# A branch prefetch hint in TensorE's stream ahead of each branch over an expert's further tiles

## The chip, the cores and the metric

The kernel runs on one core of one Trainium2 chip. The metric is the device time of one execution in microseconds (us), as the median of several runs. Five engines run their own instruction streams and meet through semaphores: TensorE (PE; its weight loads are shown apart as PEld), VectorE (DVE), ScalarE (ACT), GpSimd (POOL) and SyncE (SP, which issues most DMAs). A "q" behind an engine's name (PEq, DVEq) means its sequencer, which branches and signals and feeds the engine.

## What is computed

One layer of a decoder trunk over 2,048 tokens of width 1,024: a mixer of three kinds of heads, and then a mixture of 16 experts, of which each token uses two. The change lies in the experts:

```python
def hierarchical_moe(h, w_rg, b_rg, w_re, b_re, w_gate, w_up, w_down):
...
    top_p, top_local = lax.top_k(expert_prob, TOP_K)
    weights = group_p * top_p / jnp.sum(top_p, axis=-1, keepdims=True)
    expert_idx = group_idx * EXPERTS_PER_GROUP + top_local
...
    for e in range(N_EXPERTS):
        hidden = jax.nn.silu(h @ w_gate[e]) * (h @ w_up[e])
        y = y + combine[..., e:e + 1] * (hidden @ w_down[e])
    return y
```

The result goes through a gate and a residual sum, and a last RMS norm. How many tokens an expert gets is known only when the router has run.

## The kernel before

The first 1,155 us or so are the mixer, the output projection and the router. The router writes, for each expert, a list of its tokens to memory, and loads the 16 counts (and four counts of groups) into registers of every engine (`nreg`). Then come the experts, one after the other, in tiles of 128 tokens.

`body(e)` (L1275) computes the first two tiles of expert e without any condition. For each tile the token rows are gathered by an indirect DMA on GpSimd (`gather`, L814) into a buffer `xg`, turned by eight transposes on TensorE (`x_T`, L1195) and split into a high and a low part (`xh`, `xl`) on ScalarE and VectorE. `gates(e, t)` (L1245) multiplies them with the gate and up weights: 8 slices of the width, three products each, 24 products of 128x512 (L53) into a bank `pv` or `sc`. ScalarE and VectorE make `hid` of it, `split_h` (L1200) turns and splits that into `hh` and `hl`, and `down` (L1214) does 12 products with the down weights. The sums go to memory by an indirect scatter-add on GpSimd (`add`, L1226), whose index tile is `PI` or `PC` (both are columns of `PIC`). The last expert has its own order (`last_body`, L1334). `gates` takes an optional function `middle`, which it calls ahead of the products of slice `MID_K`, 6; its instructions then stand between the 18th and the 19th product.

`chain(e, t)` (L1399) does the tiles from the third on (t = 2 and up), if the expert has so many tokens: a condition on the count at L1403 holds the whole tile and, nested in it, the condition for the next tile, down to the 16th. Every engine takes the branch. In TensorE's program the 14 nested bodies stand one behind the other, some 95 instructions each (a product is two, the weight load and the matmul), behind them 14 short exits, one for each condition not met (a semaphore step that makes up for what the body would have signalled, and a jump), and then what follows. An expert that has no third tile so jumps from its first branch over some 1,350 instructions. An expert with more tiles falls through once per tile, and then jumps from inside the chain; its exit ends in a second, short jump over the other exits. Here experts 4, 5, 6, 8, 10 and 11 have more than two tiles (two more for 4, three for 8, one for the others), and the other ten jump at once. `fin_chain` is a chain of the same kind over the tokens of a group.

The scheduler moves work over the conditions where nothing forbids it. So the first 14 of the 24 products of the next expert's first tile stand ahead of the branch of this expert. Which of them stay behind is told by `LATE_K` and `behind`. All of this is the same in both programs.

## Time and profile before

| what | us |
| --- | --- |
| median of 3 runs (1643.43 to 1652.88) | 1648.55 |
| the profiled execution | 1652.45 |
| its span | 1650.6 |
| TensorE busy in the span | 1429.5 |
| VectorE busy | 1116.4 |
| ScalarE busy | 763.6 |
| GpSimd busy | 591.8 |

The span is the time from the first to the last instruction of the program; what lies around it makes up the rest of the execution. Times of day below, such as 1240.23, are microseconds from the span's start. An engine's idle time is given in square brackets behind the instruction that ended it, with what that instruction had waited for. "issue" stands where it waited for nothing that the profile shows. The experts' stage is the stretch from about 1155 us on.

### The profile page before, as it was taken

How to read it: one execution, taken by the hardware profiler on the slowest of the kernel's cores; microseconds unless marked ns; L12 is line 12 of the kernel's file. 1: busy time of each engine (PE TensorE's matmuls, PEld its weight loads, DVE VectorE, ACT ScalarE, POOL GpSimd, SP SyncE). 2: the span in 40 equal slices, each digit the busy share in tenths (PEclk: the TensorE clock that was granted, in tenths of full speed). 3: DMA queues.
4: the chain of work that ended last, by engine and by line, in shares of the span. 5: the costliest groups of instructions: out<-in, count | busy, mean ns of one | idle time of the engine just before them, and what ended most of it. 6: DMA issues, size and time to landing. Idle time of an engine off the chain costs nothing. (4 is left out here: it accounts for less than half of the span.)

```text
span 1650.6 us, 23125 instructions
## 1 busy us (share of the span) xinstructions
PE 1429.5 (87%) x6896; PEld 1142.4 (69%) x6896; DVE 1116.4 (68%) x3072; ACT 763.6 (46%) x1537; POOL 591.8 (36%) x618
## 2 busy tenths in 40 slices
PE   4899999989998689889979999995899997999881
PEld 4777797777787366667757777784677775777660
DVE  5767656556556798968737887887464566466664
ACT  4373235645555478778742332223243353334331
POOL 4100133011233444545342344444342335435453
PEclk9899999999999899999988999995999998999985
DMA  9448861355668755243242443234786668587845
GB/s 315 143 123 291 299 227 71 102 154 162 171 183 233 196 152 129 70 135 106 71 149 90 141 146 135 103 107 126 222 227 156 174 198 255 118 269 220 270 98 178
DMA packets 177097, 277.07 MB, mean 168 GB/s; under 512 B 31161, under 2 KB 120265, under 8 KB 176864
## 3 DMA queue, kind: packets, MB, share of 16 engines
q1 hardware_dynamic: 151184, 212.33, 41.0%
q0 software_dynamic: 25680, 62.09, 14.0%
q8 instruction: 90, 1.47, 0.4%
q14 instruction: 143, 1.17, 0.2%
HBM read 209.90 MB, written 89.03 MB: 181 GB/s over the span
## 5 line engine op out<-in xcount | busy, mean ns | idle before, releaser
L53 PE MATMUL sc<-R,R 128*128 128x512 f32 (+1 forms) x1352 | 328.1, 394 | 14.7 <-ACT R L128 5.6
L53 PEld LDWEIGHTS sc<-R,R 128*128 128x128 f32 x1352 | 250.0, 192 | 77.0 <-DVE fmx L272 8.3
L53 PE MATMUL sc<-R,yh 128*128 128x512 f32 x512 | 171.9, 416 | 19.6 <-DVE x L923 13.4
L53 PEld LDWEIGHTS sc<-R,yh 128*128 128x128 f32 x512 | 95.9, 195 | 44.2 <-DVE x L923 18.7
L814 POOL DMA_INDIRECT xg<-h_d,LT x55 | 63.3, 1151 | 167.1 <-PEq L1403 50.4
L129 DVE TENSOR_TENSOR ptlo<-tp,pthi 128x512 fp32r<-128x512 f32 (+3 forms) x163 | 99.3, 624 | 25.7 <-ACT pthi L128 24.9
L53 PE MATMUL sc<-R,fq 128*128 128x512 f32 (+3 forms) x320 | 97.5, 404 | 16.8 <-DVE fmx L272 6.4
L128 ACT ACTIVATE pthi<-tp 128x512 fp32r<-128x512 f32 (+3 forms) x163 | 85.5, 546 | 52.6 <-PE tp L293 25.6
L53 PE MATMUL sc<-R,hh 128*128 128x512 f32 x328 | 102.7, 415 | 7.6 <-ACT hh L128 5.0
L53 PE MATMUL sc<-R,yl 128*128 128x512 f32 x256 | 103.9, 407 | 0.0
L53 PE MATMUL pv<-R,xh 128*128 128x512 f32 x256 | 88.2, 424 | 13.2 <-PEq L1403 12.9
L923 DVE SCALAR_TENSOR_TENSOR x<-sc,r,x 128x512 f32<-128x512 f32 x96 | 71.7, 747 | 36.3 <-PE sc L53 28.6
L53 PE MATMUL pv<-w,xh 128*128 128x512 f32 x256 | 85.6, 411 | 9.5 <-PEq L1403 5.8
L282 POOL TENSOR_SCALAR row<-row,frs 128x640 f32<-128x640 f32 (+11 forms) x48 | 66.7, 1391 | 48.3 <-DVE frs L281 31.8
L293 PEld LDWEIGHTS tp<-ident,row 128*128 128x128 f32 x504 | 63.0, 142 | 26.3 <-issue 10.5
L293 PE MATMUL tp<-ident,row 128*128 128x128 f32 x504 | 79.9, 277 | 0.9 <-DVE fmx L278 0.5
L129 DVE TENSOR_TENSOR R<-R,R 128x512 fp32r<-128x512 f32 (+1 forms) x122 | 78.9, 699 | 0.0
L128 ACT ACTIVATE xh<-tp 128x512 fp32r<-128x512 f32 x82 | 45.3, 596 | 71.9 <-PE tp L1195 68.5
L128 ACT ACTIVATE R<-R 128x512 fp32r<-128x512 f32 (+1 forms) x130 | 73.1, 644 | 7.6 <-POOL R L1342 5.2
L53 PEld LDWEIGHTS sc<-R,fq 128*128 128x128 f32 x320 | 54.2, 197 | 32.3 <-DVE fmx L272 9.7
L53 PEld LDWEIGHTS sc<-R,hh 128*128 128x128 f32 x328 | 61.7, 196 | 21.0 <-ACT hh L128 5.6
L280 ACT ACTIVATE row<-row,fmx 128x640 f32<-128x640 f32 (+11 forms) x48 | 68.0, 1417 | 13.7 <-DVE fmx L278 9.9
(394 smaller groups left out, 3533.3 us busy)
## 6 DMA issues: line engine op xcount, KB each, us to landing
x<-in_x SPq DMA_DIRECT2D x32, 512.0 KB
x<-in_w_mod SPq DMA_DIRECT2D x32, 512.0 KB
R<-in_w_gate SPq DMA_DIRECT2D x128, 128.0 KB
R<-in_w_up SPq DMA_DIRECT2D x128, 128.0 KB
R<-in_w_down SPq DMA_DIRECT2D x32, 512.0 KB
wraw<-in_w_inT SPq DMA_DIRECT2D x24, 512.0 KB
R<-kc_d SPq DMA_DIRECT2D x80, 128.0 KB
wm<-in_w_mod SPq DMA_DIRECT2D x32, 256.0 KB
```

The costliest lines, as they stand in the source:

```text
L53: return PE.matmul(o, l, r, start=first, stop=last)
L128: return (ACT.activation(hi, src, AF.Copy), (lo_eng or V).tensor_tensor(lo, src, f32(hi), op=ALU.subtract))
L129: (lo_eng or V).tensor_tensor(lo, src, f32(hi), op=ALU.subtract))
L280: ACT.activation(row[:, 0:n], row[:, 0:n], AF.Exp, bias=ng, accum_out=rs)
L282: G.tensor_scalar(row[:, 0:n], row[:, 0:n], rs, 1.0, op0=ALU.mult, op1=ALU.mult)
L293: PE.transpose(p[:, r * 128:(r + 1) * 128], rows[r][:, j * 128:(j + 1) * 128], ident)
L814: return G.indirect_dma_start(out=dst, out_offset=None, in_=h2_d[:, :], in_offset=bass.IndirectOffsetOnAxis(ap=idx, axis=0), **(dict(bound ...
L923: V.scalar_tensor_tensor(x1[:, sl], p, r3s[t][:, g:g + 1], x1[:, sl], op0=ALU.mult, op1=ALU.add)
```

## The change

A new helper `hint(label)` puts a branch prefetch hint into TensorE's stream, for a branch that carries a label. Each condition of `chain` gets a label, `more{e}_{t}`. The hint says "LikelyTaken". For the first condition of an expert it is put into `gates(e, 1)`, the products of the second tile, at the place of `middle`. For the others it stands at the head of the body around them. The conditions of `fin_chain` and the other engines get none.

```diff
@@ body
-            gates(e, 1)
+            gates(e, 1, lambda: hint(f"more{e}_2"))
@@ last_body
-            a = gates(e, 1)
+            a = gates(e, 1, lambda: hint(f"more{e}_2"))
@@ tile_kernel
+        def hint(label):
+            tc.mark_branch_hint_location(label, "LikelyTaken", engines=[_mybir.EngineType.PE])
+
         def chain(e, t):
...
-                with tc.If(nreg[e] > t * 128):
+                with tc.If(nreg[e] > t * 128, label=f"more{e}_{t}"):
+                    if t < NT - 1:
+                        hint(f"more{e}_{t + 1}")
                     if t > 2 and e < NE - 1:
```

On TensorE, in the products of expert 0's second tile (`pv` from `R`, `xh` and `xl`): the piece of the difference around the first hint.

```order
 L53 MATMUL pv<-R_11399,xh_11721 128x512
 L53 MATMUL pv<-R_11395,xl_11724 128x512
+L1550 BRANCH_PREFETCH_HINT
 L53 MATMUL pv<-R_11396,xh_11721 128x512
 L53 MATMUL pv<-R_11400,xh_11721 128x512
```

One instruction is new, between the 18th and the 19th of the 24 products; nothing else moves. From here to the branch stand 6 products of this tile, 2 transposes of `hid`, 12 products of `down`, 8 transposes of `x_T` and 14 products of the next expert: 42.

On TensorE, at the branch of expert 0 (`w` are the next expert's weights, `xg` and `hid` belong to the third tile): the difference at the first condition and the head of its body.

```order
 L53 MATMUL pv<-w_11750,xh_11720 128x512
 L53 MATMUL pv<-w_11754,xh_11720 128x512
-L1403 COMPARE_AND_BRANCH
+L1406 COMPARE_AND_BRANCH
+L1550 BRANCH_PREFETCH_HINT
 L1195 MATMUL tp<-ident,xg_11726 128x128 x8
 L1203 MATMUL tp<-ident,hid_11743 128x128 x2
```

The branch stands where it stood (its line is now L1406), and the hint for the next condition comes right behind it, the first instruction of the body. Over the whole program TensorE has 224 rows more, all of them hints; the other four engines have the same rows in the same order.

## Rows read from the trace of the kernel before

**Rows 1.** Busy time of each engine in two stretches, up to the experts and in them. The columns are PE, PEld, DVE, ACT and POOL busy (and their instructions), the granted TensorE clock, the DMA share and GB/s.

```profile
0.00:1155.00 1155.00, 1018.23 (x5061) 821.15 (x5062) 829.32 (x2450) 581.23 (x1163) 391.27 (x472) 0.94 0.50 155
...
1155.00:1640.00 485.00, 411.31 (x1837) 321.25 (x1835) 287.13 (x623) 182.40 (x376) 200.50 (x147) 0.93 0.70 203
```

**Rows 2.** Waits of TensorE from 1155 to 1640 us: who waited for whom, us in total, times, the longest.

```profile
PE pv L53 <- PEq L1403: 20.8, 14, 3.2
PE tp L1203 <- DVEq L1403: 9.0, 2, 6.6
PE sc L53 <- DVE hl L129: 8.0, 5, 3.3
...
PE sc L53 <- ACT hh L128: 5.0, 2, 4.5
```

**Rows 3.** Line 1403 on TensorE's sequencer over the whole span: the branches with their shortest, median and longest time in ns; and the engine that waited longest for them, in us and times.

```profile
L1403 PEldq COMPARE_BRANCH  x31: 65/3363/7258, 1164.6 to 1625.1; - x31
...
  POOL xg L814: 50.4, 6
```

**Rows 4.** The same line in short windows that hold one branch each: its time in ns and its start. They belong to experts 3, 4 (three branches), 7, 9 and 13.

```profile
L1403 PEldq COMPARE_BRANCH  x1: 6981/6981/6981, 1233.1 to 1233.1; - x1
...
L1403 PEldq COMPARE_BRANCH  x1: 70/70/70, 1257.1 to 1257.1; - x1
...
L1403 PEldq COMPARE_BRANCH  x1: 65/65/65, 1266.8 to 1266.8; - x1
...
L1403 PEldq COMPARE_BRANCH  x1: 4023/4023/4023, 1276.9 to 1276.9; - x1
...
L1403 PEldq COMPARE_BRANCH  x1: 7238/7238/7238, 1364.6 to 1364.6; - x1
...
L1403 PEldq COMPARE_BRANCH  x1: 6390/6390/6390, 1446.4 to 1446.4; - x1
...
L1403 PEldq COMPARE_BRANCH  x1: 5902/5902/5902, 1557.7 to 1557.7; - x1
```

**Rows 5.** The DMA queue q8, which brings TensorE's instructions: packets, MB and share of the DMA engines, over the span, up to 1155 us, and from 1564 to 1569.4 us.

```profile
q8 instruction: 90, 1.47, 0.4%
...
q8 instruction: 40, 0.66, 0.2%
...
q8 instruction: 1, 0.02, 1.0%
```

**Rows 6.** Timeline of TensorE at the jumps of experts 0 (two rows), 3, 7, 9 and 13: start, duration, operation, count, and in brackets the idle time before it.

```profile
1166.93 0.63 PE L53 MATMUL pv<-w,xh 128*128 128x512 f32 x2
1169.68 0.47 PE L53 MATMUL pv<-w,xl 128*128 128x512 f32 x1 [2.13 <-PEq L1403]
...
1240.23 0.48 PE L53 MATMUL pv<-R,xh 128*128 128x512 f32 x1 [2.92 <-PEq L1403]
...
1372.03 0.47 PE L53 MATMUL pv<-R,xh 128*128 128x512 f32 x1 [3.19 <-PEq L1403]
...
1452.97 0.47 PE L53 MATMUL pv<-R,xh 128*128 128x512 f32 x1 [2.21 <-PEq L1403]
...
1563.79 0.47 PE L53 MATMUL pv<-R,xh 128*128 128x512 f32 x1 [1.72 <-PEq L1403]
```

**Rows 7.** The same at the jump of expert 1 (the last row ahead of it and the first behind it) and at the exit of expert 4.

```profile
1195.49 0.40 PE L53 MATMUL pv<-R,xl 128*128 128x512 f32 x1
1196.04 0.48 PE L53 MATMUL pv<-R,xh 128*128 128x512 f32 x1
...
1281.67 0.50 PE L53 MATMUL pv<-w,xh 128*128 128x512 f32 x1 [0.44 <-PEq L1403]
```

**Rows 8.** The same at the 19th and 20th product of expert 0's second tile.

```profile
1156.80 0.63 PE L53 MATMUL pv<-R,xh 128*128 128x512 f32 x2
```

**Rows 9.** Timeline of GpSimd, VectorE and TensorE around the first products of expert 8: a scatter-add is issued, VectorE waits to write its index tile again, and TensorE waits for VectorE.

```profile
1363.13 1.56 POOL L1226 DMA_INDIRECT x_d<-yc,PIC  x1 [0.30 <-issue]
...
1373.26 0.15 DVE L1316 COPY PIC<-PIC 128x1 int32<-128x1 int32 x1 [8.69 <-DMA x_d<-yc,PIC]
...
1379.10 0.66 PE L1203 MATMUL tp<-ident,hid 128*128 128x128 f32 x2 [6.59 <-DVEq L1403]
```

**Rows 10.** The chain that ended last, in order of time, behind the jump of expert 14: start, us, what.

```profile
1598.01 1.54 PE tp L1195 x8
...
1599.67 1.04 POOL xg L814
```

**Rows 11.** Timeline of TensorE a few products behind the jumps of experts 13 and 14.

```profile
1569.31 0.58 PE L53 MATMUL pv<-R,xl 128*128 128x512 f32 x1 [4.59 <-issue]
...
1595.40 0.50 PE L53 MATMUL pv<-w,xh 128*128 128x512 f32 x1 [2.51 <-issue]
```

**Rows 12.** Busy time in five short stretches, with the columns of rows 1; the granted clock is the third number from the end.

```profile
1240.80:1244.20 3.40, 3.40 (x14) 2.83 (x13) 0.90 (x2) 1.04 (x3) 2.79 (x3) 0.50 0.55 154
...
1517.30:1520.70 3.40, 3.40 (x10) 2.63 (x11) 0.58 (x2) 0.44 (x2) 2.79 (x3) 0.50 0.13 16
1541.20:1544.60 3.40, 3.40 (x9) 2.30 (x10) 0.42 (x1) 0.44 (x2) 0.00 (x0) 0.50 0.53 193
1565.10:1575.30 10.20, 5.99 (x19) 4.91 (x19) 3.24 (x6) 3.37 (x7) 2.70 (x3) 0.50 0.30 111
1595.80:1599.20 3.40, 3.40 (x14) 2.90 (x13) 1.03 (x5) 1.58 (x4) 0.00 (x0) 0.50 0.10 34
```

## The prediction

> The timeline tells what such a wait costs TensorE [rows 6]. Branches of 6.98, 7.24, 6.39 and 5.90 us (experts 3, 7, 9, 13) leave TensorE idle 2.92, 3.19, 2.21 and 1.72 us: each time about 4.1 us less. That is the work queued ahead of the branch when the sequencer reaches it. The first branch leaves 2.13. An exit of 4.02 us, at expert 4, leaves only 0.44 us: there the cover is enough, and 0.44 is what the exit's semaphore step and its second, short branch cost anyway [rows 4, 7].

> **The change part by part.** It adds 224 hints, on TensorE alone; no other engine's instructions move. 25 are executed: 16 in the second tile's products and 9 at the head of a body that runs (31 branches, less 16 long exits, less 6 short second branches at experts 4, 5, 6, 8, 10 and 11, are 9 that fell through). 16 of them name a branch that is taken, 9 one that isn't.

> *The hint itself.* No row of before shows one. The nearest is a sequencer instruction that goes nowhere, the branch not taken at 65 to 70 ns: 25 x 0.07 = 1.8 us of the sequencer, which runs some 4 us ahead of TensorE [rows 4, 6]. I take 0; the bounds are 0 and 1.8. Without that cover it would cost the 1.8.

> *Is it early enough?* Between the hint and the branch of an expert stand 42 products. TensorE starts the first of them at 1156.80 for expert 0, and the last two ahead of the jump at 1166.93 [rows 8, 6]: 10.1 us for a fetch that took at most 7.3. In a body the hint stands right behind one branch, and the next branch comes 9.7 us later (1257.1, 1266.8) [rows 4]. So a fetch that starts at the hint, or even 2.4 us behind it, is in place.

> *What goes.* All the exposed time down to what a near jump leaves. That floor is 0.44 us for the six exits from inside a chain, and about 0.15 for the eight others (expert 1, whose wait is wholly covered, has one product end at 1195.49 + 0.40 and the next start at 1196.04) [rows 7]. 20.8 - 6 x 0.44 - 8 x 0.15 = 17.0 us. Bounds: 0 (the hint does nothing) and 17.0.

> *What is late next.* Behind expert 7's branch TensorE waits 6.59 us for VectorE, which sat 8.69 us on the landing of a scatter-add that GpSimd had issued at 1363.13, before that branch [rows 9]. This wait doesn't move with TensorE, so the 3.0 us of that branch (3.19 - 0.15) come back as a longer wait: -14.0 left. For the others I see the queued work follow TensorE: GpSimd's gathers behind the branch wait 50.4 us for TensorE's sequencer [rows 3], and the chain that ended last goes through TensorE's transposes behind expert 14's branch and the gather that they release [rows 10].

> *The code that moves.* Two more holes carry the name "issue": 4.59 us at 1569.31 and 2.51 us at 1595.40 [rows 11], a few products behind the jumps of experts 13 and 14. In the first, one packet of q8 falls between jump and the hole's end [rows 5]: the block behind the target is not there yet. TensorE had run 10,123 instructions in 40 blocks by 1155 us [rows 1, 5], 253 each. The holes put a block's end some 12 and 3 instructions behind the two targets. In the changed program 196 and 210 more instructions stand ahead of these, which puts the next block's end some 70 and 45 behind the targets. At 0.23 us a pair of weight load and product that is 8 and 5 us of work, as long as most fetches. Both holes should close: -7.1 us. Other jumps come nearer to a block's end (expert 6, from some 115 to some 20 instructions), for which I give back 2. Taken: -5; bounds -7.1 and +2 (the two holes only move to other experts).

> *The clock.* [...] The bounds are 0 (the clock falls elsewhere) and -9.8. I take -6, as idle times of up to 6.6 us for VectorE stay.

> *Sum.* -14.0 - 5 - 6 = -25. TensorE has 22 us of other waits in the stage (9.0 + 8.0 + 5.0, and small ones) [rows 2]; I let 3 come back through them. So -22 us. The profiled execution took 1652.45 us (its span 1650.6), which becomes 1630.45. The median of the three runs is 1648.55, 3.9 lower; the gain is a difference within one execution, so I set it against the median: 1648.55 - 22 = 1626.5.

> **The rivals.**
> *A. The hint fetches nothing of use* (it is ignored, or it fetches the place where the branch falls through, which comes next anyway). Branches stay at 3.4 to 7.3 us, and only the moved code counts: 1648.55 - 5 = 1643.5, from 1641.5 to 1650.5. For it: no row shows a hint, and the body is the branch's "true" side. Against it: nothing in the rows.
> *B. The jumps get short, but what follows isn't ready.* Besides expert 7's, the holes of experts 0 and 3 are followed by waits of 3.3 us (for hl, the longest of its line) and 2.4 us (the smaller of the two on VectorE's queue) [rows 2]. If these only grow, the 2.0 and 2.8 us of those holes come back too, and with clock and code as before -14.0 + 4.8 = -9.2 is left, or 1639.5. Against it: VectorE's part ahead of both starts from TensorE's transposes.
> *C. Slower: the block that a hint fetches takes the place of the one that comes next.* Counted in blocks of some 255 instructions, a block's end lies between hint and branch at experts 0, 1, 2, 3 and 12 of the ten that jump at once, and nine hints are wrong. Each of these 14 then has a fetch more in its way. At the five, the second fetch finds the queued work already used up, and costs near the middle of 3.4 and 7.3 us [rows 3], say 5: +25. The nine find their 4.1 us of cover: +1 each, +9. The jumps that still win give -9, the moved code -5: +20, or 1668.5. It decides against the change once the 14 cost more than 14 us together, 1 us each. For it: up to 1155 us the trace has one block per 253 instructions, so no row shows that more than the next one is kept [rows 5]. Against it: in 9.7 us between hint and branch there is time for two fetches one behind the other.
> [...]

> **How the numbers follow.** Forecast 0.60, A 0.16, B 0.12, C 0.12. A measurement of this kernel can tell about 0.5%, 8.2 us, from no change: faster is below 1640.3, slower above 1656.8. Faster: 0.56 of the forecast, 0.03 of A (its lower end with a little of the jumps), 0.06 of B, together 0.65. Slower: 0.11 of C and 0.01 of A, 0.12. The rest, 0.23, is within. The range: the forecast's own bounds are 1648.55 - 17.0 - 7.1 - 9.8 = 1614.6 below, and B's 1639.5 above. I reach up to 1650 to hold A, and down to 1612, and leave out C and a little of the forecast's edge.

> **What would show it.** In the profile after, right: the 16 exits at L1406 take 0.1 to 0.3 us, TensorE's wait for its sequencer there falls from 20.8 to under 5 us, q8 has more packets than 90 (nine wrong hints), no "issue" hole of over 2 us stands behind experts 13 and 14, and fewer stretches have a clock of 0.50. A: the exits keep their 3.4 to 7.3 us. B: short exits, but the waits for hl and on VectorE's queue grow by as much. C: exits and "issue" holes that together cost more than the 20.8 + 7.1 us of now. I am wrong if the exits are short and the stage from 1155 us on still takes as long.

## The result and the profile after

The changed kernel took 1658.70 us (median of 8 runs, 1651.24 to 1661.05) against 1648.7 of the kernel before on the same chip: 1.0058 times its time, interval 1.0037 to 1.0079. The forecast was 1626.5, with a range up to 1650. The profiled execution took 1659.7 us, its span is 1657.3.

The waits of TensorE in the experts' stage (1155 to 1645 us; who waited for whom, us in total, times, the longest) answer to [rows 2]:

```profile
PE tp L1203 <- DVEq L1406: 24.2, 8, 10.9
PE sc L53 <- DVE hl L129: 11.6, 4, 5.1
PE tp L1203 <- DVE hid L1263: 6.6, 1, 6.6
PE pv L53 <- ACT xh L128: 5.9, 4, 5.3
PE sc L53 <- ACT hh L128: 5.1, 3, 4.0
PE pv L53 <- PEq L1406: 5.1, 8, 2.3
...
PE pv L53 <- issue: 0.2, 1, 0.2
```

Read the sixth row first: the wait for TensorE's own sequencer, 20.8 us before, is 5.1. The "issue" holes of [rows 11] are gone too (7.1 to 0.2). But the wait for VectorE's sequencer at the same branch has grown from 9.0 us to 24.2, and those for hl, hid and xh have grown as well (from 8.0, 3.5 and 1.4 us). All rows of this view add to 63.8 us, where those of before add to 60.1: TensorE is idle for longer than before, for other engines.

The branch's line over the whole span, and who waited for it (us, times), against [rows 3]:

```profile
L1406 PEldq COMPARE_BRANCH  x31: 69/327/6477, 1165.0 to 1630.5; - x31
...
  PE tp L1203: 24.2, 8
...
  DVE hid L1263: 5.9, 1
```

The same line in windows that hold experts 3, 4, 7, 9 and 13, against [rows 4]:

```profile
L1406 PEldq COMPARE_BRANCH  x1: 327/327/327, 1237.8 to 1237.8; - x1
...
L1406 PEldq COMPARE_BRANCH  x3: 69/78/338, 1258.7 to 1278.7; - x3
...
L1406 PEldq COMPARE_BRANCH  x1: 350/350/350, 1368.6 to 1368.6; - x1
...
L1406 PEldq COMPARE_BRANCH  x1: 6477/6477/6477, 1450.8 to 1450.8; - x1
...
L1406 PEldq COMPARE_BRANCH  x1: 364/364/364, 1561.6 to 1561.6; - x1
```

So here the hint does what it says: 14 of the 16 exits take 0.33 to 0.38 us, and the 16 together 13.3 us, after 81.4. Expert 0's took 1.86 us, and expert 9's stayed at 6.48. The packets of q8 over the span and from 1247.0 to 1258.6 us, and those of q14, the other queue that the profile calls "instruction", answer to [rows 5]:

```profile
q8 instruction: 81, 1.33, 0.3%
...
q8 instruction: 1, 0.02, 0.5%
...
q14 instruction: 144, 1.18, 0.2%
```

That q8 serves TensorE is read from the trace of before: in each of the 16 long branches falls a packet of q8, of 16,384 bytes. Queue q8 moved fewer packets than before, 81 after 90, although nine hints are wrong; q14 moved 143 before. At expert 4 one packet comes behind the first hint, at 1251.6, none from the second hint (1258.8) to the branch of the exit, and this branch, at 1278.7, takes 338 ns. I read this as one fetch that served all three hints: the exit blocks of one expert lie close together in the program.

Where some of the time went is to be seen at expert 7, in the timelines of GpSimd, VectorE and TensorE, against [rows 9]:

```profile
1367.14 1.56 POOL L1226 DMA_INDIRECT x_d<-yc,PIC  x1 [0.30 <-issue]
...
1378.55 0.15 DVE L1316 COPY PIC<-PIC 128x1 int32<-128x1 int32 x1 [9.97 <-DMA x_d<-yc,PIC]
...
1384.38 0.66 PE L1203 MATMUL tp<-ident,hid 128*128 128x128 f32 x2 [10.93 <-DVEq L1406]
```

TensorE's hole of 3.19 us at this exit is gone, and the one behind it is 10.93 us, not 6.59. That much the prediction had. What it had not is on the other engines. The next four fences give the same line, 1403 or 1406, in ScalarE's program at expert 3's exit and in VectorE's at expert 13's, in a second trace of the kernel before and in the changed kernel: the branch, and the first semaphore step in the block that it jumps to, each with its start at the end of the row.

```profile
L1403 ACTq COMPARE_BRANCH  x1: 45/45/45, 1230.1 to 1230.1; - x1
L1403 ACTq EVENT_SEMAPHORE  x1: 17/17/17, 1230.8 to 1230.8; - x1
```

```profile
L1406 ACTq COMPARE_BRANCH  x1: 45/45/45, 1228.6 to 1228.6; - x1
L1406 ACTq EVENT_SEMAPHORE  x1: 17/17/17, 1231.2 to 1231.2; - x1
```

```profile
L1403 DVEq COMPARE_BRANCH  x1: 63/63/63, 1554.8 to 1554.8; - x1
L1403 DVEq EVENT_SEMAPHORE  x1: 21/21/21, 1555.6 to 1555.6; - x1
```

```profile
L1406 DVEq COMPARE_BRANCH  x1: 56/56/56, 1561.8 to 1561.8; - x1
L1406 DVEq EVENT_SEMAPHORE  x1: 21/21/21, 1567.7 to 1567.7; - x1
```

On these engines the branch itself is short, 45 to 63 ns here, and the wait stands between it and the first step of the block behind. ScalarE's exit went from 0.7 to 2.6 us, VectorE's from 0.8 to 5.9, though neither has a hint or a different instruction. From branch to semaphore step, VectorE's 16 exits add to 34.8 us before and 49.0 after (36.7 and 46.5 in the second traces, runs 5 and 6). I read these waits as fetches, as on TensorE. The packets of q14 don't tell for which engine they came, but the traces speak for it: in the 18 traces of this case every exit of VectorE and ScalarE that took over 0.5 us more than the engine's own work in it, 173 in all, has a packet of q14 in it, and of the other 403 only 49 have one. (In the traces of before and of the changed kernel these are 18 of 18, and 4 of the other 46.) The short exits, such as VectorE's of 0.72 us, hold 0.68 us of work.

These exits are where TensorE's new waits stand. In the trace of before TensorE waits for VectorE's sequencer at experts 4 and 7 alone. In the changed kernel it does so at expert 0 (1.26 us) and at experts 5, 10, 11, 12 and 13 as well, for 2.05, 2.08, 2.08, 2.48 and 1.25 us. At these five VectorE's exits went from 0.7, 0.7, 0.7, 2.5 and 0.8 us to 2.8, 2.8, 2.8, 4.9 and 5.9. Expert 10 as an example, VectorE before, then VectorE and TensorE after (the second branch of the row is the short one over the other exits):

```profile
L1403 DVEq COMPARE_BRANCH  x2: 47/52/56, 1482.9 to 1483.7; - x2
L1403 DVEq EVENT_SEMAPHORE  x1: 21/21/21, 1483.6 to 1483.6; - x1
```

```profile
L1406 DVEq COMPARE_BRANCH  x2: 47/52/56, 1486.8 to 1489.7; - x2
L1406 DVEq EVENT_SEMAPHORE  x1: 21/21/21, 1489.6 to 1489.6; - x1
...
1489.77 0.41 PE L1203 MATMUL tp<-ident,hid 128*128 128x128 f32 x2 [2.08 <-DVEq L1406]
```

### The profile page after: what moved, and what is told of

Read it like the earlier page. It is cut to its first block, busy times and chain, and to the rows that moved or that the text cites. A ratio compares the mean times of both kernels' runs of the same rounds, so it can differ in the third digit from the quotient of the medians.

```text
span 1657.3 us, 23150 instructions
## 1 busy us (share of the span) xinstructions
PE 1430.2 (86%) x6896; PEld 1140.7 (69%) x6896; DVE 1117.7 (67%) x3072; ACT 763.6 (46%) x1537; POOL 592.3 (36%) x618
## 3 DMA queue, kind: packets, MB, share of 16 engines
q14 instruction: 144, 1.18, 0.2%
## 5 line engine op out<-in xcount | busy, mean ns | idle before, releaser
L53 PEld LDWEIGHTS sc<-R,fq 128*128 128x128 f32 x320 | 55.6, 202 | 31.3 <-DVE fmx L272 11.2
```

The lines of the kernel that those rows point to most:

```text
L53: return PE.matmul(o, l, r, start=first, stop=last)
```

## The experiments

Theory 1: TensorE's exit no longer ends last, and other engines set the pace; Theory 1b adds that VectorE's index copies, which wait for scatter-adds, hide the gain. Theory 2: the change moves the other engines' programs against the pieces in which they are fetched (the packets of q14, of 8,192 bytes: 1.18 MB in 144); Theory 2b says that the blocks named in hints do this. Theory 3: hints, wrong ones above all, cost time themselves. Ratios are to the kernel before on the same chip. The number in a run's label is the run's number here; in the expectations e0 to e15 without more are the experts.

**Runs 1 to 4: which hints, on which engine.** `e1_layout` executes none; the edit puts 14 hints for the deepest exit into its body:

```diff
-                    if t < NT - 1:
-                        hint(f"more{e}_{t + 1}")
+                    if t == NT - 2:
+                        for _ in range(14):
+                            hint(f"more{e}_{t + 1}")
```

and `gates(e, 1)` without a hint.

> All 14 hints of an expert stand together in the body of its deepest tile, which never runs; no hint is executed, and TensorE's program is as long as in the changed kernel. Theory 1 (another engine's exit now ends last, and the hints do only what they say): as before, 1643 to 1653 us, TensorE's long exits 3.4 to 7.3 us again, VectorE's exits long at the experts where they were before (e0, e3, e9). Theory 2 (224 more instructions move the other engines' programs against the pieces in which they are fetched): VectorE's exits are long at e1, e10 to e13 as in the changed kernel (4.7 to 5.9 us against 0.7), though no hint runs, and the time is over before, 1655 to 1670 us. Theory 3 (executed hints cost): as before.

Measured: 1650.96 us, 1.0026 (1.0004 to 1.0048). TensorE's exits are long again, VectorE's are near those of before (36.0 us in all), but at experts 10 and 11 they are 2.9 and not 0.7. Length alone, as Theory 2 had it, doesn't do it: TensorE's program is as long as in the changed kernel, and the pattern of exits isn't that one's. But this run too names 16 blocks, the deepest exit of each expert, so its 0.26% isn't the price of length alone.

`e2_pe_vector` adds hints on VectorE, behind its index copy and in the bodies:

```diff
-            V.tensor_copy(PC[e % 4], none)
+            c = V.tensor_copy(PC[e % 4], none)
+            with after([c]):
+                hint(f"more{e}_2", "DVE")
...
                     if t < NT - 1:
                         hint(f"more{e}_{t + 1}")
+                        hint(f"more{e}_{t + 1}", "DVE")
```

> TensorE's hints as in the changed kernel, and the same hints on VectorE: ahead of an expert's first branch and in the bodies. Theory 1: VectorE's exits fall to 0.7 us (what it takes to drain) wherever they were 2.5 to 5.9, the 24.2 us that TensorE's transposes waited for VectorE's queue fall under 12, and the time under before: 1628 to 1642 us. Theory 2: the same, if VectorE's fetches are hidden wherever its program lies: 1628 to 1642 us. Theory 3 (a hint itself costs the engine that runs it): slower than the changed kernel, over 1660 us.

Measured: 1653.83 us, 1.0044 (1.0023 to 1.0065), the changed kernel again. The hints on VectorE (the row of its 25, then q14 over the span, then the exit of expert 13):

```profile
L1555 DVEq BRANCH_PREFETCH_HINT  x25: 39/39/56, 1146.1 to 1622.0; - x25
...
q14 instruction: 144, 1.18, 0.2%
...
L1410 DVEq COMPARE_BRANCH  x1: 61/61/61, 1555.2 to 1555.2; - x1
L1410 DVEq EVENT_SEMAPHORE  x1: 21/21/21, 1560.8 to 1560.8; - x1
```

25 of them ran and brought no packet more (144, as in the changed kernel); the exit took 5.6 us with its hint. As placed here, the hint shows no effect on VectorE, so Theory 1 could not be tried this way. Why, is open.

`e3_vector_only` is the same without TensorE's hints.

> VectorE's hints alone, none on TensorE. Theory 1 (TensorE's exit was the bound before, VectorE's is next): TensorE's exits 3.4 to 7.3 us as before, VectorE's 0.7; little gain, 1640 to 1650 us. Theory 2: VectorE's exits were short at most experts before, so little changes: 1643 to 1652 us. If VectorE was the bound all along: under 1640 us.

Measured: 1655.39 us, 1.0062 (1.0040 to 1.0085), outside every expectation: slower, with no hint on TensorE and none of use on VectorE. ScalarE's exit at expert 3 took 3.1 us here too, though no instruction was added to ScalarE or TensorE. What this run has in common with the changed kernel is the list of blocks that its hints name.

`e4_first_only` keeps the hint ahead of an expert's first branch and drops those in the bodies.

> TensorE's hint ahead of an expert's first branch alone (16 in all), none within the bodies. Theory 1: as the changed kernel, 1652 to 1661 us, TensorE's exits 0.3 us at the experts with two tiles, and VectorE's long exits at e1, e5, e10 to e13 as there. Theory 2: 208 instructions fewer, so VectorE's program lies against its pieces nearly as before: its exits at e1, e10 to e13 are 0.7 to 2.5 us again, and the time falls under before, 1632 to 1645 us. Theory 3 (wrong hints in the bodies evict or delay): under before as well, but with VectorE's exits long as in the changed kernel.

Measured: 1648.42 us, 1.0007 (0.9986 to 1.0029). TensorE's 16 exits take 13.1 us, the longest 6.2 at expert 11, and expert 9's is short; ScalarE's at expert 3 is 0.7 again, VectorE's add to 40.1 us. So some of the loss went with the hints in the bodies.

**Runs 5 and 6: the two kernels again.** No edit.

> The kernel before once more, unchanged, for a second trace of it. If the place of VectorE's program against the pieces in which it is fetched (Theory 2) decides which of its exits are long, the long ones stand at e0, e3, e4, e9 again and nowhere else; if they depend on what the run has just fetched, other experts show them, and single exits of one trace carry no reading. Time 1643 to 1653 us.

> The changed kernel once more, unchanged. Theory 2: VectorE's long exits again at e0, e1, e9, e12, e13 (4.7 to 5.9 us) and 2.8 at e4, e5, e10, e11. Otherwise some of them move. Time 1651 to 1661 us, TensorE's exits short as before but for e0 and e9.

Measured: 1649.01 us, 1.0003 (0.9986 to 1.0020), and 1656.43 us, 1.0052 (1.0032 to 1.0072). VectorE's exits of 4 us and more stand where they stood: before at experts 0, 3 and 9 (4.9, 6.7 and 5.7 us), changed at experts 1, 9, 12 and 13 (5.8, 5.6, 4.4 and 5.6); expert 0's is 3.1 for 5.7. TensorE's exit of expert 9 takes 6.6 us again. Which exits wait belongs to the program, then, and a single trace carries that reading; how long one waits varies more.

**Runs 7 and 8: index copies that don't wait.** The copies stood three experts ahead of their use in VectorE's program, right behind a scatter-add that read the same column:

```diff
-            V.tensor_copy(PC[e % 4], none)
+            with after(last[-1:]):
+                V.tensor_copy(PC[e % 4], none)
             tc.keep_in_program_order(V.tensor_copy(PI[e % 4], lt[:, 1, 0:1]))
```

> No hints. VectorE's two index copies of an expert (lines 1316 and 1317) stand behind its own low parts of the hidden rows, not three experts early, where they wait for a scatter-add that has just been issued (18.2 us before, longest 8.7, with weight splits and low parts queued behind them). Theory 1b (TensorE's exit is hidden since the products behind it wait for VectorE, and VectorE for the landing of GpSimd's scatter-adds): that wait is gone, some of it shows: 1636 to 1645 us. Rival (VectorE's wait is hidden, and its own exit fetch sets the pace): as before, 1643 to 1653 us.

> The same with all of the change's hints. Theory 1b: with VectorE free of the landing, TensorE's short exits are worth what they save, 8 to 16 us less than the kernel of the run before: 1622 to 1635 us. Rival: no better than that kernel, or over 5 us worse as the change itself was, 1645 to 1660 us.

Measured: 1641.12 us, 0.9962 (0.9942 to 0.9981), and with all hints 1635.90 us, 0.9932 (0.9912 to 0.9952). VectorE has no wait of its index copies left. With these copies the change is worth 0.3%, uncertain by 0.3%, and no longer costs 0.6%. Theory 1b wanted 8 to 16 us more from the hints; they gave 5.

**Runs 9 and 10: blocks named, no hint executed.** The decisive pair. All 14 hints of an expert, each for its own block, stand in the body of the deepest tile:

```diff
-                    if t < NT - 1:
-                        hint(f"more{e}_{t + 1}")
+                    if t == NT - 1:
+                        for u in range(2, NT):
+                            hint(f"more{e}_{u}")
```

The compiled programs of VectorE, ScalarE, GpSimd and SyncE are then, to the byte, those of the changed kernel. Against the kernel before they differ in one mark at the head of each of the 224 blocks that a hint names.

> All 14 hints of an expert, each with its own target, stand in the body of the deepest tile, which never runs: no hint is executed, but every exit block is the target of one, as in the changed kernel, and the programs of VectorE, ScalarE and GpSimd are the changed kernel's. Theory 2b (a block that a hint names lies differently in the program of every engine, so others' exits become long): ScalarE's exits at e3 and e14 take 2.6 to 3.7 us, GpSimd's at e8 1.8, VectorE's at e1, e12, e13 4.4 to 5.9 and at e5, e10, e11 2.8, as in the changed kernel, TensorE's stay 3.4 to 7.3 us as before, and the time is over the changed kernel's: 1660 to 1675 us. Rival (the executed hints lengthen the others' exits, by their fetches): VectorE's and ScalarE's exits as before, 1643 to 1653 us.

> The same with the late index copies, no hint executed. Theory 2b: over the late copies alone by what the long exits of the others cost, 1645 to 1660 us, and over the late copies with hints by what TensorE's short exits save, 8 to 20 us. Rival: as the late copies alone, 1636 to 1646 us.

Measured: 1662.68 us, 1.0077 (1.0052 to 1.0101); with late copies 1643.31 us, 0.9959 (0.9939 to 0.9979). In the first, two of TensorE's waits, and ScalarE's exit at expert 3:

```profile
PE tp L1203 <- DVEq L1406: 18.3, 7, 8.7
PE pv L53 <- PEq L1406: 17.7, 14, 3.3
...
L1406 ACTq COMPARE_BRANCH  x1: 45/45/45, 1231.9 to 1231.9; - x1
L1406 ACTq EVENT_SEMAPHORE  x1: 17/17/17, 1234.8 to 1234.8; - x1
```

ScalarE waits 2.9 us, VectorE's exits add to 45.9 us, TensorE's are as long as before, and no hint has run: naming the blocks, without a hint executed, costs 0.77%, 12.7 us. TensorE's own program has 224 rows more than before here; run 1 has as many, names 16 blocks and costs 0.26%, so some 0.5%, uncertain by 0.3%, goes with the 208 other blocks. Theory 2b holds here. In the second TensorE's wait for its sequencer is 21.8 us and no time is lost against the late copies alone, which Theory 2b had not expected: there VectorE's exits grow by 3.6 us only (36.5 to 40.1).

**Runs 11 and 12: fewer blocks.** Late copies with the first hints alone, and with one right hint for each expert:

```diff
+        MORE = {4: 2, 5: 1, 6: 1, 8: 3, 10: 1, 11: 1}
...
-                    if t < NT - 1:
+                    if t == MORE.get(e, 0) + 1:
                         hint(f"more{e}_{t + 1}")
```

> Late index copies, and the hint ahead of each expert's first branch alone: 16 blocks are named, not 224. Theory 2b: fewer of the others' exits become long, ScalarE's and GpSimd's none, and TensorE's stay short: 3 to 10 us under the late copies with all hints, 1625 to 1633 us. Rival (the hints in the bodies cost nothing and change nothing): as with all hints, 1633 to 1640 us.

> Late index copies, and one hint for each expert, ahead of the branch that is taken with these inputs, so that no hint is wrong. Theory 2b: 16 blocks named as in the run before, other ones at e4, e5, e6, e8, e10, e11, and VectorE's long exits move with them; time 1625 to 1635 us. Theory 3 (wrong hints cost): under the run before by 1 us for each of the nine wrong ones.

Measured: 1631.83 us, 0.9892 (0.9861 to 0.9923), and 1633.75 us, 0.9912 (0.9885 to 0.9940). The first is the fastest median of all runs, 16.8 us under the kernel before on its chip. The first still runs six wrong hints, at the six experts with more than two tiles, and not nine as the expectation of run 12 has it; at 1 us each they would cost 0.36%. Leaving them out gave 0.20% the other way, uncertain by 0.4%: Theory 3, at that price, falls.

**Runs 13 and 14: what the 16 hints save.** One hint for each expert, naming its first exit, in the deepest body:

```diff
-                        for u in range(2, NT):
-                            hint(f"more{e}_{u}")
+                        hint(f"more{e}_2")
```

> One hint for each expert, naming the exit block of its first branch as in the run with the first hints alone, but standing in the deepest body, which never runs: no hint is executed, and the programs of VectorE, ScalarE and GpSimd are that run's (1648.4 us, 1.0007 of before). What its hints save is this run less that one. Theory 1b (the saving is hidden while VectorE waits for the scatter-adds): about the same time, 1646 to 1653 us. Theory 2b alone (the saving is real everywhere, and was eaten by the others' exits): TensorE's exits 3.4 to 7.3 us again and 10 to 17 us more, 1658 to 1666 us.

> The same with the late index copies, against the run with late copies and first hints (1631.8 us, 0.9892 of before). Theory 1b: with VectorE free of the landing the saving shows, so this run is 8 to 14 us over that one, 1640 to 1646 us. Theory 2b alone: the same saving as with the early copies. If the hints save nothing in either, this run is at 1630 to 1634 us.

Measured: 1654.53 us, 1.0030 (1.0003 to 1.0056), and 1636.18 us, 0.9937 (0.9910 to 0.9965). Four pairs now hold the other engines' programs fixed, and their difference is what running the hints saves: 224 blocks 1.0077 - 1.0055 (mean of the two) = 0.22%, with late copies 0.9959 - 0.9932 = 0.27%; 16 blocks 1.0030 - 1.0007 = 0.23%, with late copies 0.9937 - 0.9892 = 0.45%. On average 0.29%, some 5 us, each pair uncertain by about 0.3 to 0.4%. That late copies free more of it, as Theory 1b had it, isn't shown.

Where the rest goes is to be read from the last pair. First run 14, then run 11:

```profile
PE pv L53 <- PEq L1407: 17.5, 12, 3.9
...
PE tp L1203 <- DVEq L1407: 2.5, 2, 2.1
```

```profile
PE tp L1203 <- DVEq L1407: 12.0, 5, 4.9
PE tp L1195 <- DMA xg<-h_d,LT: 6.9, 4, 2.7
PE pv L53 <- PEq L1407: 4.6, 7, 2.3
```

TensorE's wait for its own sequencer falls by 12.9 us, and that for VectorE's grows by 9.5. All of TensorE's waits in the stage: 49.4 to 42.8, so 6.6 us are left; in the pair of run 9 and the changed kernel 68.2 to 63.8, and in the pairs of runs 10 and 8 and of runs 13 and 4 53.2 to 44.7 and 66.6 to 55.6. VectorE's own exit ends next: at experts 7, 12 and 13 its semaphore step comes 1.1, 0.6 and 0.1 us behind TensorE's in run 14, and 5.3, 3.8 and 1.5 us in run 11.

**Runs 15 and 16: what a named block moves.** First hints at experts 9 to 15 alone, with early and late copies:

```diff
-            gates(e, 1, lambda: hint(f"more{e}_2"))
+            gates(e, 1, (lambda: hint(f"more{e}_2")) if e > 8 else None)
```

> Early index copies as before, and the first hint at experts 9 to 15 alone: 7 blocks named, none of them ahead of expert 9. Theory 2b with the reading that a named block moves the code behind it: every exit of VectorE up to e8 is as before (0.7 us at e1, 5.5 to 6.7 at e3), and only later ones differ; TensorE's exits from e9 on are 0.3 us, and the time is 2 to 6 us under before, 1641 to 1647 us. Rival (named blocks change the whole program's place): VectorE's exit at e1 is long here too, as with 16 named.

> The same with the late index copies. Theory 2b: VectorE's exits up to e8 as with the late copies alone (0.7 us at e1, 2.5 at e7, against 4.5 and 6.5 with 16 named), and TensorE's long exits up to e8 come back; time 1628 to 1636 us, within 4 us of the late copies with all first hints (1631.8). Rival: VectorE's exits at e1 and e7 long as there, 1633 to 1640 us.

Measured: 1648.66 us, 0.9992 (0.9971 to 1.0014), and 1635.11 us, 0.9906 (0.9875 to 0.9937). The first gains nothing that shows, where 2 to 6 us were expected. VectorE's exit of expert 1 in run 15, then in run 4, where 16 blocks are named:

```profile
L1406 DVEq COMPARE_BRANCH  x1: 56/56/56, 1189.8 to 1189.8; - x1
L1406 DVEq EVENT_SEMAPHORE  x1: 21/21/21, 1190.5 to 1190.5; - x1
```

```profile
L1406 DVEq COMPARE_BRANCH  x1: 56/56/56, 1185.7 to 1185.7; - x1
L1406 DVEq EVENT_SEMAPHORE  x1: 21/21/21, 1190.6 to 1190.6; - x1
```

With no block named ahead of expert 9, the long and the short exits of experts 0 to 8 are those of before, on VectorE and ScalarE (expert 3's is long again, at 3.2 us, but shorter than the 5.5 and 6.7 of before); behind that one of VectorE's differs (expert 11: 2.8 us for 0.7). With late copies likewise: experts 1 and 7 are at 0.7 and 2.5 us, as with the late copies alone, and not at 4.5 and 6.5 as in run 11. So in these two runs a named block acted on the exits behind it, not on those ahead. In the compiled programs the code stands in the same rows and only the mark differs. By what means the mark lengthens an exit is not shown: the traces hold no addresses.

## Why the prediction was wrong

*What goes* was right: 20.8 us of TensorE's waits at its own branches became 5.1 (2.3 of what is left at expert 9), 15.7 of the 17.0 forecast. *The hint itself* costs nothing that shows: 25 of 31 to 41 ns. *Is it early enough* was right for 14 of 16, but the fetch seems to start later than the 2.4 us that I had allowed: the first packet of q8 comes 6.9, 3.7 and 5.5 us behind the hints of experts 1, 2 and 3, and 10.8 us behind that of expert 0, whose exit still took 1.86 us. Expert 9's exit stayed long in both traces of the changed kernel (6.48 and 6.60 us) and is short in run 4, where the bodies hold no hints. In the changed kernel no packet of q8 falls between that expert's hint and its branch (1441.5 to 1450.8 us); the one packet comes at 1454.8, during the branch. Why no packet follows that hint is open.

*The code that moves* closed the two "issue" holes, -6.9 us, as worked out, where -5 was taken. They are gone in run 9 too, where no hint runs, so it is the moved code that closed them.

*The clock* gave nothing: the stretches with a granted clock of 0.50 behind 1155 us add to 80.8 us before (84.1 in its second trace) and 84.0 after, and the stage's mean is 0.93 in both. The stretches stand elsewhere now (expert 13's 10.2 us are 3.4, and 3.4 us are new at 1319.9, 1490.6 and 1524.7), but TensorE's idle time is no less, and neither is the low clock. That is 6 us of the sum. No run shows these 6 us, nor the 9.8 of their bound; what the traces show is a 128x512 product every 0.43 us at a granted clock of 0.50 and every 0.23 us at 1.00.

The step that failed is *What is late next*, with the first sentence of the part, "on TensorE alone; no other engine's instructions move". It gave back 3 us at expert 7 and 3 more for all else. In the traces all of TensorE's waits in the stage other than those at its own branches and in the two holes went from 32.2 to 58.5 us (34.5 to 59.7 between the second traces): 26.3 us came back, more than the 22.6 us that had gone. Two things stood in its place. First, naming blocks in hints acted on the exits of the other engines: some of VectorE and ScalarE that had been short are long now, with a packet of q14 in them (VectorE's of expert 1, 4.7 us for 0.7; ScalarE's of expert 3, 2.6 for 0.7), and GpSimd's of experts 8, 12 and 14 went from 0.4 us to 1.9, 2.7 and 2.5, while fewer became short (VectorE's of expert 3, ScalarE's of expert 15, GpSimd's of expert 9). The naming costs 12.7 us, shown by run 9 with no hint executed; that it does so through these exits is read from TensorE's waits for VectorE's sequencer there (18.3 us for 9.0). The order of instructions, which I had compared, cannot show that. Second, even with those programs fixed, the hints save some 5 us, not 14 to 17. "The queued work follows TensorE" is what I had argued from GpSimd's waits; I had not looked at VectorE's own exits, though the trace of before holds them: there its exit ended 0.6 to 1.3 us ahead of TensorE's at experts 0, 3, 9 and 11, and behind it at eight others (semaphore step against semaphore step). That is rival B's mechanism, larger than the 3.3 and 2.4 us that I had set for it, and at more experts: the wait on VectorE's queue went from 9.0 to 24.2. B took TensorE's late work as its cause, not VectorE's own exits. (B's sum is 1639.35, not 1639.5, which changes nothing.)

Rival C, with the right sign, had the wrong mechanism: at expert 4 one packet was all that came up to the exit behind three hints, and leaving the wrong hints out gained nothing that shows (0.9892 in run 11, 0.9912 in run 12). How much of its program TensorE holds at a time no run here shows; at expert 4 the branch of the exit took 0.34 us, 27 us and two hints behind that packet. Rival A is excluded by the exits.

The arithmetic as measured, in per cent of the time before: +0.77 for the named blocks, -0.22 (uncertain by 0.3) for the hints in this pair, +0.55, or 9 us, in place of -22.

## What to carry to other kernels

When several engines take the same branch, shortening one engine's exit gained here only until the next engine's exit ended (from run 14 to run 11 TensorE's wait for its own sequencer fell by 12.9 us, and that for VectorE's grew by 9.5): line up all of them, branch to first step behind, before pricing one. Here a hint was not local to the engine that runs it (0.77% slower in run 9, with none executed); compare it with a kernel that names the same blocks and executes no hint, and name as few as do the work (16 came out cheaper than 224 in all four comparisons here, in one of them within the noise). Here the sure gain lay elsewhere, in a copy that sat three experts early behind a scatter-add's landing (-0.4% alone, -1.1% with the first hints).

## What the runs showed of the hardware that was new

From the branch to the first step behind it, an exit took VectorE up to 6.7 us (expert 3 in run 5) and ScalarE up to 4.7 (expert 15, before), against 0.7 and 0.4 at the shortest; TensorE's branch itself took 3.3 (run 10) to 7.8 us (run 14) with no hint executed. In the second traces of both kernels VectorE's exits of 4 us and more stand at the same experts, but for expert 0's in the changed kernel (3.1 us for 5.7). Ahead of 14 of 16 exits a hint on TensorE went with a branch of 0.33 to 0.38 us; on VectorE, 25 hints of 39 to 56 ns brought no packet more, and expert 13's exit took 5.6 us behind its hint, 5.9 without one.
